# Gated-MLP down projection as Strassen products of halves, interleaved with the up projection, in a one-core decoder layer

## Chip, cores and metric

One NeuronCore of a Trainium2 chip runs the whole layer in one launch. The metric is the device time of the program in microseconds (us). TensorE is written PE, its weight loads PEld, VectorE DVE, ScalarE ACT, GpSimd POOL and SyncE SP, as in the profile.

## The reference

With DEPTH = 1 there is one layer: attention with forget gates (FoX), a layer norm, a gated MLP with a causal depthwise convolution of three taps, a second layer norm, and a gated embedding. There are 512 tokens, the model width is 1024, the inner width of the MLP 2816. Everything is float32.

```python
def conv_ffn(x, w_up, conv_w, conv_b, w_down):
    u, g = jnp.split(x @ w_up, [FFN_DIM], axis=-1)
    g = causal_dwconv(g, conv_w, conv_b)
    return (jax.nn.gelu(g, approximate=False) * u) @ w_down

x = layer_norm(ALPHA * x + fox_mixer(x, ...), ln_mix_g, ln_mix_b)
x = layer_norm(ALPHA * x + conv_ffn(x, ...), ln_ffn_g, ln_ffn_b)
x = x + sigmoid(x @ ple_w_gate + ple_b_gate) * (p @ ple_w_proj)
```

## The kernel before, in words

**Split operands.** Each float32 operand is held as two fp32r tiles, hi and lo, and each product is three matmuls into one PSUM bank: hi·hi, hi·lo, lo·hi (`three`, L93; the matmul is L98). ACT writes hi as a copy, DVE writes lo as the difference. For the weights the class `Weights` does this: `load_to` (L59) issues a DMA of a unit of 128x1024 on SP's queue into one of 4 raw buffers, `cut_to` (L70) makes `whi` on ACT (L77) and `wlo` on DVE (L78) in one of 6 pairs of buffers (`SPLIT_BUFS`), and `get` (L82) cuts some units ahead and loads some more. Units are used in the order in which they were added.

**Order of the work.** The code is written in the order of the work, and a scheduler of the framework sets the final order of each engine's instructions from it; each engine then takes its own in that order. PSUM has eight banks, given out by `bank` (L103).

**Attention** (L345 to L410) ends with the output projection. Its second half of columns (`ap`, L468 to L480) goes over four token tiles t = 0..3 of 128 tokens. After each tile DVE adds the residual and takes statistics, and `norm` (L437) normalizes the row, with POOL's power in the middle. `flip` (L449) then turns a tile: eight PE transposes into two banks `nt`, which ACT and DVE read out as `x1h` (L458) and `x1l` (L459). `flip(t - 2)` stands after tile t, so tiles 2 and 3 are still to be flipped when the loop ends. Between them and the MLP stand seven embedding products (`pl`, L496 to L503, six matmuls each), and the last two flips are laid between those.

**The MLP** (L506 to L565) goes through the 22 inner tiles f in two parts of 11. For each f it makes g and u (24 matmuls of 512 columns each), then ACT and DVE do the convolution and the gelu (L520 to L525), DVE multiplies (`e`, L527) and ACT and DVE split the result into `hh`, `hl` (L528, L529). After the 11 tiles of a part comes its down projection: for each half n of the output's columns, 11 inner tiles x 4 token tiles x 3 matmuls, `d`, each with 128 tokens as stationary operand and 512 columns moving. Four banks hold the four token tiles. `add_half` (L425) adds a bank to `y`, the running row. In the last quarter the token tile is the outer loop, and `norm` and `flip` of the second layer norm follow tile by tile.

**The gate** (L568 to L601) multiplies the flipped rows with the gate weights (`gt`), 24 matmuls for each of 8 outputs; the last one is done in two halves of 256 columns, with its embedding product last.

The body of the loop that the change replaces is this:

```python
for k in range(FH):
    for t in range(NT):
        step(t, k)
for t in range(NT):
    add_half(t, n, acc[t], part == 0)
```

Of the kernel before, what the change touches and what calls it, by code (L numbers as in the profile page):

```python
# [15 lines left out]
P = 128  # L16
S = 512
# [8 lines left out]
FH = NF // 2  # L26
# [11 lines left out]
SPLIT_BUFS = 6  # L38
# [7 lines left out]
class Weights:  # L46
# [8 lines left out]
    def add(self, src, n=UNIT, inner=None):  # L55
        self.units.append((src, n, inner))
        return len(self.units) - 1

    def load_to(self, i):  # L59
        while self.loaded < min(i, len(self.units)):  # L60
            src, n, inner = self.units[self.loaded]
# [4 lines left out]
            self.nc.sync.dma_start(v, src)  # L66
            self.raw[self.loaded] = t
            self.loaded += 1

    def cut_to(self, i):  # L70
        while self.cut < min(i, len(self.units)):
            self.load_to(self.cut + 1)
            n = self.units[self.cut][1]
            t = self.raw.pop(self.cut)
            hi = self.pool.tile([P, UNIT], F32R, tag="whi", name=f"whi{self.cut}", bufs=SPLIT_BUFS)
            lo = self.pool.tile([P, UNIT], F32R, tag="wlo", name=f"wlo{self.cut}", bufs=SPLIT_BUFS)
            self.nc.scalar.activation(hi[:, :n], t[:, :n], AF.Copy)  # L77
            self.nc.vector.tensor_sub(lo[:, :n], t[:, :n], hi[:, :n].bitcast(F32))  # L78
            self.parts[self.cut] = (hi, lo)
            self.cut += 1  # L80
# [8 lines left out]
def trunk_layer(ctx: ExitStack, tc: tile.TileContext, xT, x2d, pT, wqk, wv0, wv1, wv2, bf, wo, wup, cwb,  # L89
# [3 lines left out]
    def three(ps, whi, wlo, xhi, xlo, start, stop, weights_move=False, lo_first=False):  # L93

        pairs = ((wlo, xhi), (whi, xlo), (whi, xhi)) if lo_first else ((whi, xhi), (whi, xlo), (wlo, xhi))
        for n, (w, x) in enumerate(pairs):
            lhsT, rhs = (x, w) if weights_move else (w, x)
            nc.tensor.matmul(ps, lhsT, rhs, start=start and n == 0, stop=stop and n == 2)  # L98

    base = ctx.enter_context(tc.tile_pool(name="base", bufs=1))  # L100
    psum = ctx.enter_context(tc.tile_pool(name="psum", bufs=8, space=bass.MemoryType.PSUM))

    def bank(name):  # L103
        return psum.tile([P, 512], F32, tag="b", name=name)
# [25 lines left out]
    u_p = W.add(pT.rearrange("(k p) t -> p k t", p=P), inner=S)  # L130
    u_pl = [W.add(half_rows(wpl, 0, 2, n), inner=512) for n in range(2)]
    u_up, u_dn = [], {}
    for part in range(2):
        for f in range(part * FH, (part + 1) * FH):
            u_up.append([W.add(wup[f, s], inner=P) for s in (1, 0)])
        for n in range(2):
            k0 = part * FH
            u_dn[part, n] = []
            for j in range(0, FH, 2):
                c = min(2, FH - j)  # L140
                u_dn[part, n].append(W.add(half_rows(wdn, k0 + j, c, n), n=c * 512, inner=512))
    u_g = [[W.add(half_rows(wg, 2 * j, 2, n), inner=512) for j in range(4)] for n in range(2)]
    tl = slice(S - P, S)
# [271 lines left out]
    def row(src, name):  # L415
        t = post.tile([P, D], F32, tag="row", name=name, bufs=2)
        nc.sync.dma_start(t, src[0:1, :].to_broadcast([P, D]))
        return t

    g1, b1 = row(gm, "g1"), row(bm, "b1")  # L420
# [16 lines left out]
    def norm(t, g, b):  # L437
        mv = post.tile([P, 4], F32, tag="mv", name="mv", bufs=2)
        nc.vector.bn_aggr(mv[:, 0:2], stats.pop(t))
        nc.vector.tensor_scalar_add(mv[:, 2:3], mv[:, 1:2], EPS)  # L440
        nc.gpsimd.tensor_tensor(mv[:, 3:4], mv[:, 2:3], neghalf, op=ALU.pow)  # L441
        for n in range(2):
            c = slice(n * 512, (n + 1) * 512)
            nc.vector.scalar_tensor_tensor(y[:, t, c], y[:, t, c], mv[:, 0:1], g[:, c],
                                           op0=ALU.subtract, op1=ALU.mult)
            nc.vector.scalar_tensor_tensor(y[:, t, c], y[:, t, c], mv[:, 3:4], b[:, c],
                                           op0=ALU.mult, op1=ALU.add)
# [14 lines left out]
    x1l = post.tile([P, KD, S], F32R, tag="xl", name="x1l")  # L462

# [4 lines left out]
    for t in range(NT):  # L468
# [10 lines left out]
        if t > 1:  # L479
            flip(t - 2, x1h, x1l)  # L480
    oT.close()


    pl = base.tile([P, NT, D], F32, tag="xl", name="pl")
    W.cut_to(u_p + 3)
# [10 lines left out]
    for i, (n, t) in enumerate([(n, t) for n in range(2) for t in range(NT)][:-1]):  # L496
# [3 lines left out]
        if i == 1:  # L500
            flip(2, x1h, x1l)
        if i == 4:
            flip(3, x1h, x1l)  # L503


    hpool = ctx.enter_context(tc.tile_pool(name="hpool", bufs=1, side="right"))  # L506
    g2 = b2 = x2h = x2l = None
    for part in range(2):
        hh = hpool.tile([P, FH, S], F32R, tag="hh", name=f"hh{part}")
        hl = hpool.tile([P, FH, S], F32R, tag="hl", name=f"hl{part}")  # L510
        for fl in range(FH):
            f = part * FH + fl
            pg, pu = bank(f"g{f}"), bank(f"u{f}")
            for ps, u in ((pg, u_up[f][0]), (pu, u_up[f][1])):
                hi, lo = W.get(u, 2)
                for k in range(KD):
                    c = slice(k * P, (k + 1) * P)
                    three(ps, hi[:, c], lo[:, c], x1h[:, k, :], x1l[:, k, :], k == 0, k == KD - 1)
            a = hpool.tile([P, S], F32, tag="a", name=f"a{f}", bufs=2)
            nc.scalar.activation(a, pg, AF.Identity, bias=cw[:, f, 3:4], scale=cw[:, f, 2:3])  # L520
            nc.vector.scalar_tensor_tensor(a[:, 1:], pg[:, :S - 1], cw[:, f, 1:2], a[:, 1:],
                                           op0=ALU.mult, op1=ALU.add)
            nc.vector.scalar_tensor_tensor(a[:, 2:], pg[:, :S - 2], cw[:, f, 0:1], a[:, 2:],
                                           op0=ALU.mult, op1=ALU.add)
            nc.scalar.activation(a, a, AF.Gelu)  # L525
            e = hpool.tile([P, S], F32, tag="e", name=f"e{f}", bufs=2)
            nc.vector.tensor_mul(e, a, pu)  # L527
            nc.scalar.activation(hh[:, fl, :], e, AF.Copy)  # L528
            nc.vector.tensor_sub(hl[:, fl, :], e, hh[:, fl, :].bitcast(F32))  # L529
        if part == 1:  # L530
            g2, b2 = row(gf, "g2"), row(bff, "b2")
            x2h = post.tile([P, KD, S], F32R, tag="xh", name="x2h")
            x2l = post.tile([P, KD, S], F32R, tag="xl", name="x2l")
        for n in range(2):
            us = u_dn[part, n]
            last = part == 1 and n == 1
            acc = {}

            def step(t, k, us=us):
                hi, lo = W.get(us[k // 2])  # L540
                c = slice(k % 2 * 512, k % 2 * 512 + 512)
                tk = slice(t * P, (t + 1) * P)
                three(acc[t], hi[:, c], lo[:, c], hh[:, k, tk], hl[:, k, tk], k == 0, k == FH - 1,
                      weights_move=True)

            if not last:
                for t in range(NT):
                    acc[t] = bank(f"d{part}{n}{t}")
                for k in range(FH):
                    for t in range(NT):  # L550
                        step(t, k)
                for t in range(NT):
                    add_half(t, n, acc[t], part == 0)
                    if part == 1:
                        half_stats(t, n)
            else:
                for t in range(NT):
                    acc[t] = bank(f"d{part}{n}{t}")
                    for k in range(FH):
                        step(t, k)  # L560
                    add_half(t, n, acc[t], False)
                    half_stats(t, n)
                    norm(t, g2, b2)
                    if t > 1:
                        flip(t - 2, x2h, x2l)  # L565


    bgs = row(bg, "bgs")  # L568

    def gate(n, t, lo_c=0, w=512):  # L570
# [8 lines left out]
        e = hpool.tile([P, S], F32, tag="e", name=f"ge{n}{t}", bufs=2)[:, :w]  # L579
# [10 lines left out]
    for n in range(2):  # L590
        for t in range(NT - n):
            if n == 0 and t == 1:
                flip(2, x2h, x2l)
            if n == 0 and t == 2:
                flip(3, x2h, x2l)
            finish(n, t, gate(n, t), pl[:, t, n * 512:(n + 1) * 512])
    es = [gate(1, NT - 1, c, 256) for c in (0, 256)]
    for e, c in zip(es, (0, 256)):
        ps = bank(f"pl{NT - 1}_1{c}")[:, :256]
        embed(ps, u_p1, u_pl1, 0, P, c, 256)  # L600
        finish(1, NT - 1, e, ps, c, 256)  # L601
# [48 lines left out]
```

## Time and profile before

| | us |
|---|---|
| three timed runs | 671.20, 671.52, 672.05 |
| median | 671.52 |
| the profiled execution | 671.42 |
| its span, first to last instruction | 669.40 |
| around the span | 2.02 |

The profile is of one execution. Its page gives the busy time of each engine and the chain that ended last; the trace behind it gives each instruction with its start and duration. A matmul's record lasts longer than its slot, since matmuls are pipelined: the step from one start to the next is what one costs, and the duration (0.39 us for 512 columns) is not.

### The profile page before, as it was taken

The page shows a single profiled execution, that of the slowest core. Times are in us where ns is not written, and L with a number is a line of the kernel's source. Part 1 is how long each engine was busy: PE and PEld are TensorE (multiplying, and loading weights), DVE is VectorE, ACT ScalarE, POOL GpSimd, SP SyncE. Part 2 cuts the span into 40 slices and gives each one's busy share as a digit, 9 for nine tenths or more (in the row PEclk, how much of TensorE's full clock was granted, in tenths as well). Part 3 has the DMA queues.
Part 4 walks back from the last instruction along what each step waited for, and adds up shares of the span by engine and source line. Part 5 has one row for each costly group of instructions (what it writes and reads, how often), then busy time and mean ns, then how long its engine had stood idle before and what let it go on. Part 6 is the DMA issues. An engine that isn't in the chain of part 4 may idle for free.

```text
span 669.4 us, 8448 instructions
## 1 busy us (share of the span) xinstructions
PE 663.2 (99%) x3216; PEld 562.9 (84%) x3216; DVE 400.7 (60%) x642; ACT 290.3 (43%) x497; POOL 80.8 (12%) x78
## 2 busy tenths in 40 slices
PE   9999999999999999999999999999999999999997
PEld 7899888888888888888888888888888888888886
DVE  6774789999895796444545323254444543268763
ACT  6644687777775155343433212133343432104331
POOL 0000555444553010000000000000000000001000
PEclk9999999999999999999999999999999999999999
DMA  8533212211251317222232323233222222212411
GB/s 290 185 128 127 63 65 65 65 40 59 65 208 44 129 63 252 95 94 95 94 95 79 94 80 124 95 118 101 97 94 95 94 80 95 78 64 65 163 48 48
DMA packets 27880, 67.50 MB, mean 101 GB/s; under 512 B 2560, under 2 KB 6400, under 8 KB 27840
## 3 DMA queue, kind: packets, MB, share of 16 engines
q1 hardware_dynamic: 27840, 66.97, 30.2%
q8 instruction: 25, 0.41, 0.2%
q14 instruction: 15, 0.12, 0.1%
HBM read 64.73 MB, written 2.10 MB: 100 GB/s over the span
## 4 chain that ended last, share of the span: by engine, by line
PE 97%; ACT 1%; DMA 1%; SPq 0%; issue 0%; DVE 0%; DVEq 0%
PE d L98 18%; PE g L98 18%; PE u L98 18%; PE pp L98 13%; PE gt L98 7%; PE pv L98 6%; PE ao L98 3%; PE ap L98 3%; PE o L333 3%; PE t L320 2%; PE pl L98 2%; PE s L289 1%; PE s L291 1%; PE nt L454 1%; DMA raw<-wv 1%
## 5 line engine op out<-in xcount | busy, mean ns | idle before, releaser
L78 DVE TENSOR_TENSOR wlo<-raw,whi 128x1024 fp32r<-128x1024 f32 (+4 forms) x118 | 135.6, 1154 | 154.0 <-ACT whi L77 151.7
L77 ACT ACTIVATE whi<-raw 128x1024 fp32r<-128x1024 f32 (+4 forms) x118 | 118.4, 1005 | 207.0 <-PE g L98 82.8
L307 POOL TENSOR_SCALAR pr<-pr,rl 128x128 f32<-128x128 f32 (+1 forms) x64 | 72.7, 1153 | 134.2 <-DVE rl L303 134.2
L98 PE MATMUL d<-whi,hh 128*128 128x512 f32 x176 | 68.6, 390 | 0.0
L98 PE MATMUL d<-wlo,hh 128*128 128x512 f32 x176 | 68.5, 389 | 0.0
L98 PE MATMUL d<-whi,hl 128*128 128x512 f32 x176 | 68.5, 389 | 0.0
L98 PE MATMUL g<-x1h,whi 128*128 128x512 f32 x176 | 68.5, 389 | 0.0
L98 PE MATMUL g<-x1h,wlo 128*128 128x512 f32 x176 | 68.5, 389 | 0.0
L98 PE MATMUL u<-x1l,whi 128*128 128x512 f32 x176 | 68.5, 389 | 0.0
L98 PE MATMUL g<-x1l,whi 128*128 128x512 f32 x176 | 68.5, 389 | 0.0
L98 PE MATMUL u<-x1h,wlo 128*128 128x512 f32 x176 | 68.5, 389 | 0.0
L98 PE MATMUL u<-x1h,whi 128*128 128x512 f32 x176 | 68.5, 389 | 0.0
L441 POOL TENSOR_TENSOR mv<-mv,neghalf 128x1 f32<-128x1 f32 x8 | 7.3, 913 | 406.2 <-DVE mv L440 384.0
L98 PE MATMUL pp<-xh,wlo 128*128 128x512 f32 x128 | 50.2, 392 | 0.0
L98 PE MATMUL pp<-xl,whi 128*128 128x512 f32 x128 | 50.0, 391 | 0.0
L98 PE MATMUL pp<-xh,whi 128*128 128x512 f32 x128 | 49.9, 390 | 0.0
L527 DVE TENSOR_TENSOR e<-a,u 128x512 f32<-128x512 f32 x22 | 15.1, 688 | 43.5 <-PE u L98 41.4
L299 ACT ACTIVATE pr<-s,nm 128x128 f32<-128x128 f32 (+1 forms) x64 | 33.4, 525 | 16.9 <-DVE nm L298 14.8
L98 PEld LDWEIGHTS g<-x1l,whi 128*128 128x128 f32 x176 | 33.0, 188 | 6.9
L98 PEld LDWEIGHTS u<-x1l,whi 128*128 128x128 f32 x176 | 33.0, 188 | 6.9
L98 PEld LDWEIGHTS d<-whi,hh 128*128 128x128 f32 x176 | 33.0, 188 | 6.9
L98 PEld LDWEIGHTS g<-x1h,whi 128*128 128x128 f32 x176 | 33.0, 188 | 6.9
(129 smaller groups left out, 1254.2 us busy)
## 6 DMA issues: line engine op xcount, KB each, us to landing
raw<-wup SPq DMA_DIRECT2D x44, 512.0 KB
raw<-wdn SPq DMA_DIRECT2D x20, 512.0 KB
raw<-wqk SPq DMA_DIRECT2D x16, 512.0 KB
raw<-wo SPq DMA_DIRECT2D x8, 512.0 KB
raw<-wg SPq DMA_DIRECT2D x8, 512.0 KB
raw<-wv SPq DMA_DIRECT2D x8, 384.0 KB
y<-x2d SPq DMA_DIRECT2D x4, 512.0 KB
xraw<-xT SPq DMA_DIRECT2D x7, 256.0 KB
```

The costliest lines, as they stand in the source:

```text
L77: self.nc.scalar.activation(hi[:, :n], t[:, :n], AF.Copy)
L78: self.nc.vector.tensor_sub(lo[:, :n], t[:, :n], hi[:, :n].bitcast(F32))
L98: nc.tensor.matmul(ps, lhsT, rhs, start=start and n == 0, stop=stop and n == 2)
L289: nc.tensor.matmul(ps[:, :n], QA[:, q], KA[:, :n], start=True, stop=False)
L291: nc.tensor.matmul(ps[:, :n], qb[0:68, q], kb[0:68, :n], start=False, stop=True)
L299: nc.scalar.activation(pr[:, off:off + w], ps[:, :w], AF.Exp, bias=nm[:, i:i + 1], accum_out=ls[:, i:i + 1])
L307: nc.gpsimd.tensor_scalar_mul(pr[:, off:off + w], pr[:, off:off + w], rl[:, i:i + 1])
L320: nc.tensor.transpose(ps[:, w:w + P], pr[:, o:o + P], ident)
L333: nc.tensor.matmul(ps[:, q0:], V[:, j, h], p[:, o:o + w], start=j == 0 and n == 0, stop=j == NT - 1 and n == 1)
L441: nc.gpsimd.tensor_tensor(mv[:, 3:4], mv[:, 2:3], neghalf, op=ALU.pow)
L454: nc.tensor.transpose(ps[:, k * P:(k + 1) * P], y[:, t, (4 * n + k) * P:(4 * n + k + 1) * P], ident)
L527: nc.vector.tensor_mul(e, a, pu)
```

## The change

**Down projection.** The inner tiles are now taken in pairs (2j, 2j+1). For a pair, the rows of the activations are cut into two halves of 256 tokens and the weights into two halves of 512 output columns, so that the pair's product is a 2x2 by 2x2 product of blocks. For 9 of the 11 pairs this is done with seven block products instead of eight, in Winograd's form of Strassen's scheme. The left operands are A11, A22, A12 and four sums S1 to S4, which DVE makes in float32 from the four blocks before they are split (`operands`; split with one ACT and one DVE instruction of 128x1792). The right operands are two blocks as they are and T1 to T4, which DVE makes in the raw weight buffers before they are split (`make` in `down_units`). For T1 and T2 a block of the weights is loaded a second time into a tile `side`. The last two pairs (inner tiles 18 to 21, `REST`) are done as before.

**Order.** There are four parts of 6, 6, 6 and 4 inner tiles. The down products of a part (12 chunks: nine of two products, i.e. 12 matmuls, and three of one, i.e. 6 matmuls) are run between the g and u of the next part (`between`, `CHUNKS`): one chunk after each in parts 1 and 2, two and one by turns in part 3. The six banks x, y, z (two each) hold the running sums; some are read into `y` by DVE and go on accumulating.

**Banks.** The eight-bank pool of attention is closed after the first layer norm's loop, and a new pool with six banks and two for g and u is opened.

**The first tiles.** The embedding products no longer stand between the first layer norm and the MLP, but between the second and the gate. `flip(2)` now follows `flip(1)` at once, and g and u of tile 0 and g of tile 1 are made in halves of 256 tokens: first the tokens 0 to 255, then `flip(3)`, then the others.

**The rest.** `SPLIT_BUFS` is 5 instead of 6. `norm` works on 1024 columns in one instruction instead of two of 512. The second norm takes its token tiles in the order 2, 3, 0, 1.

```diff
-SPLIT_BUFS = 6
+PAIRS = (range(0, 3), range(3, 6), range(6, 9))
+REST = range(18, 22)
+CHUNKS = (None, (1,) * 12, (1,) * 12, (2, 1) * 4)
+HALF = S // 2
+SPLIT_BUFS = 5
...
+            for piece in [t[:, :n]] if make is None else make(t):
+                e = c + piece.shape[-1]
+                self.nc.scalar.activation(hi[:, c:e], piece, AF.Copy)
+                self.nc.vector.tensor_sub(lo[:, c:e], piece, hi[:, c:e].bitcast(F32))
+                c = e
...
+                t1, t2 = t[:, :512], side[part][:, i, :]
+                nc.vector.tensor_sub(t1, t1, t2)
+                nc.vector.tensor_sub(t2, t[:, 512:], t1)
+                return [t1, t2]
...
+            nc.vector.tensor_sub(t[:, :512], t[:, 512:], t[:, :512])
+            return [t]
...
+                nc.vector.tensor_sub(t[:, :512], t[:, :512], side[part][:, i, :])
+                return [t[:, :512]]
...
+    first.close()
+    psum.append(ctx.enter_context(tc.tile_pool(name="psum2", bufs=6, space=bass.MemoryType.PSUM)))
...
+        nc.vector.tensor_add(s1, a21, a22)
+        nc.vector.tensor_sub(s2, s1, a11)
+        nc.vector.tensor_sub(s3, a11, a21)
+        nc.vector.tensor_sub(s4, a12, s2)
+        nc.scalar.activation(hh[:, i], E[:, HALF:], AF.Copy)
+        nc.vector.tensor_sub(hl[:, i], E[:, HALF:], hh[:, i].bitcast(F32))
...
+        phases = ((ua, (("x", A11, 0), ("y", A12, 1)), (("x", 0, 0), ("y", 0, 0))),
+                  (ub, (("z", S1, 0), ("x", S2, 1)), (("x", 0, 1), ("z", 1, 1))),
+                  (uc, (("x", S3, 0), ("z", S4, 1)), (("x", 1, 1), ("z", 0, 1))),
+                  (ud, (("x", A22, 0),), (("x", 1, 0),)))
...
+    flip(2, x1h, x1l)
...
+            if f == 0:
+                a, b = slice(0, HALF), slice(HALF, S)
+                up(0, 0, a)
+                up(0, 1, a)
+                flip(3, x1h, x1l)
+                up(1, 0, a)
+                up(0, 0, b)
+                up(0, 1, b)
+                up(1, 0, b)
...
+            if f > 1:
+                up(f, 0)
+            conv(f)
+            between()
+            up(f, 1)
+            product(f, E[:, q * S:(q + 1) * S])
+            if q:
+                if part < 3:
+                    operands(hh, hl, j - 3 * part, E)
...
+            between()
+        if part < 3:
+            before = down(part, hh, hl)
```

The change moves instructions at two places that matter below. The first is PE's order where attention hands over to the MLP. Here `ap` is the last product of attention, `nt` the transposes of a flip, `pl` an embedding product, `g` the first product of the MLP. Before:

```order
L98 MATMUL ap_2582<-wlo_2465,oh 128x512
L454 MATMUL nt<-ident,y 128x128 x8
L98 MATMUL pl_0_2641<-whi_2633,whi_2476 128x512
L98 MATMUL pl_0_2641<-whi_2633,wlo_2477 128x512
L98 MATMUL pl_0_2641<-wlo_2634,whi_2476 128x512
```

And after the change:

```order
L115 MATMUL ap_2579<-wlo_2468,oh 128x512
L518 MATMUL nt<-ident,y 128x128 x16
L115 MATMUL g_2652<-x1h,whi_2479 128x256
L115 MATMUL g_2652<-x1l,whi_2479 128x256
L115 MATMUL g_2652<-x1h,wlo_2480 128x256
```

The twelve embedding matmuls that stood between the flip of tile 1 and that of tile 2 are gone: the 16 transposes are both flips, one behind the other, and the first half product of the MLP follows.

DVE's order at the same place: `y<-y,mv` are the norm of tile 2, `wlo` weight splits, `y<-y,ap` the residual of tile 3, `BN_STATS` its statistics and `x1l` what reads the banks of the flip of tile 1 out. Before:

```order
L444 SCALAR_TENSOR_TENSOR y<-y,mv,g_2407 128x512 x2
L446 SCALAR_TENSOR_TENSOR y<-y,mv,b_2409 128x512 x2
L78 TENSOR_TENSOR wlo_2638<-raw_2468,whi_2637 128x1024
L428 SCALAR_TENSOR_TENSOR y<-y,ap_2582 128x512
L78 TENSOR_TENSOR wlo_2693<-raw_2480,whi_2692 128x1024
L435 BN_STATS st_2437<-y 128x6
L459 TENSOR_TENSOR x1l<-nt,x1h 128x4x128
L439 BN_AGGR mv<-st_2437 128x2
L459 TENSOR_TENSOR x1l<-nt,x1h 128x4x128
```

And after the change:

```order
L510 SCALAR_TENSOR_TENSOR y<-y,mv,g_2414 128x1024
L94 TENSOR_TENSOR wlo_2654<-raw_2459,whi_2653 128x1024
L511 SCALAR_TENSOR_TENSOR y<-y,mv,b_2416 128x1024
L94 TENSOR_TENSOR wlo_2658<-raw_2471,whi_2657 128x1024
L496 SCALAR_TENSOR_TENSOR y<-y,ap_2579 128x512
L523 TENSOR_TENSOR x1l<-nt,x1h 128x4x128
L503 BN_STATS st_2440<-y 128x6
L523 TENSOR_TENSOR x1l<-nt,x1h 128x4x128
```

It is the same work but for the small aggregate, with the weight splits one row earlier.

The third place is DVE in part 3, between the chunks of the last Strassen part. `wlo` are weight splits, `raw` the differences that make a right operand in a raw buffer as soon as its load has landed (L174 for T3, L181 for T4), `a` the convolution, `E` the product with u, `y<-y,z` and `y<-y,x` the reading of the running sums:

```order
L94 TENSOR_TENSOR wlo107_4739<-raw107_4666,whi107_4738 128x1024
L570 SCALAR_TENSOR_TENSOR a19_4692<-g19_4657,cw_2407,a19_4692 128x511
L572 SCALAR_TENSOR_TENSOR a19_4692<-g19_4657,cw_2407,a19_4692 128x510
L94 TENSOR_TENSOR wlo108_4772<-raw108_4701,whi108_4771 128x1024
L174 TENSOR_TENSOR raw111_4776<-raw111_4776 128x512
L94 TENSOR_TENSOR wlo109_4797<-raw109_4723,whi109_4796 128x1024
L181 TENSOR_TENSOR raw113_4836<-raw113_4836,side2_4565 128x512
L577 TENSOR_TENSOR E9_4516<-a19_4692,u19_4737 128x512
L498 TENSOR_TENSOR y_2210<-y_2210,z20_4555 128x512
L94 TENSOR_TENSOR wlo110_4833<-raw110_4742,whi110_4832 128x1024
L680 TENSOR_TENSOR hl3_4515<-E9_4516,hh3_4514 128x1024
L498 TENSOR_TENSOR y_2210<-y_2210,x20_4557 128x512
```

None of these rows but the splits, the convolution and the product stood in the order before, where one row per weight unit and four per inner tile went through DVE here.

More of the change, by code (lines that the diff above doesn't have):

```diff
@@ L129, in trunk_layer @@
     u_o = [[W.add(half_rows(wo, 2 * j, 2, n), inner=512) for j in range(4)] for n in range(2)]
[L130 to L141, printed above, removed]
+    side = {}
@@ L480, in trunk_layer, with up @@
             flip(t - 2, x1h, x1l)
+    rows.close()
     oT.close()
+    first.close()
+    psum.append(ctx.enter_context(tc.tile_pool(name="psum2", bufs=6, space=bass.MemoryType.PSUM)))
+    hpool = ctx.enter_context(tc.tile_pool(name="hpool", bufs=1, side="right"))
+    ups = {}
+    def up(f, s, c=slice(0, S)):
+        if (f, s) not in ups:
+            ups[f, s] = bank(f"{'gu'[s]}{f}", *(() if f < 6 else ("gu", 2)))
+        hi, lo = W.get(u_up[f, s], 2)
+        for k in range(KD):
+            w = slice(k * P, (k + 1) * P)
+            three(ups[f, s][:, c], hi[:, w], lo[:, w], x1h[:, k, c], x1l[:, k, c], k == 0, k == KD - 1)
@@ new lines, in trunk_layer @@
+    gb = hpool.tile([P, 2, D], F32, tag="E", name="g2b2")
+    g2, b2 = row(gb[:, 0, :], gf), row(gb[:, 1, :], bff)
+    x2h = post.tile([P, KD, S], F32R, tag="xh", name="x2h")
+    x2l = post.tile([P, KD, S], F32R, tag="xl", name="x2l")
+    for g in ("hh", "hl"):
+        extra.append(hpool.tile([P, 3, UNIT], F32R, tag=g, name=f"{g}p", bufs=2))
+    for i, t in enumerate(tiles):
+        tk = slice(t * P, (t + 1) * P)
+        for n in range(2):
+            ps = bank(f"r{t}_{n}")
+            for k in range(len(REST)):
+                hi, lo = W.get(u_r[n][k // 2])
+                c = slice(k % 2 * 512, k % 2 * 512 + 512)
+                three(ps, hi[:, c], lo[:, c], hh[:, k, tk], hl[:, k, tk], k == 0, k == len(REST) - 1,
+                      weights_move=True)
+            add_half(t, n, ps, False)
+            half_stats(t, n)
+        norm(t, g2, b2)
+        if i == 0:
+            W.cut_to(u_pl[1] + 1)
+        if i > 1:
+            flip(tiles[i - 2], x2h, x2l)
@@ L494, in embed @@
             three(ps, hi[:, c], lo[:, c], ph[:, pk], plo[:, pk], k == 0, k == 1, weights_move=True)
[L496 removed]
+    for i, (n, t) in enumerate([(n, t) for n in range(2) for t in tiles][:-1]):
         ps = bank(f"pl{t}_{n}")
@@ L499, in trunk_layer @@
         nc.scalar.activation(pl[:, t, n * 512:(n + 1) * 512], ps, AF.Copy)
[L500 to L565, printed above, removed]
@@ L568, in trunk_layer @@
-    bgs = row(bg, "bgs")
+        if i == 3:
+            flip(0, x2h, x2l)
+    bgs = row(hpool.tile([P, D], F32, tag="hl", name="bgs", bufs=2), bg)
     def gate(n, t, lo_c=0, w=512):
```

183 lines of the change are left out of this document (148 added, 35 removed).

## The prediction

> **What bounds the kernel now.** I read the page first, then the chain, then PE's waits, then PE's steps.
>
> ```profile
> span 669.4 us, 8448 instructions
> PE 663.2 (99%) x3216; PEld 562.9 (84%) x3216; DVE 400.7 (60%) x642; ACT 290.3 (43%) x497; POOL 80.8 (12%) x78
> PE 97%; ACT 1%; DMA 1%; SPq 0%; issue 0%; DVE 0%; DVEq 0%
> ```
>
> ```profile
> PE warm L153 <- DVE zeros L149: 1.1, 1, 1.1
> PE pv L98 <- ACT whi L77: 0.5, 1, 0.5
> ```
>
> PE is busy for 99% of the span, the chain is PE for 97%, and the list of PE's waits has two entries, both in the first ten microseconds. A busy share can hide slow matmuls, so the step counts: in the chain, 264 down matmuls in a row, and in PE's timeline the first and the last of twelve matmuls of 256 columns at the end.
>
> ```profile
> 376.70 59.84 PE d L98 x264
> ```
>
> ```profile
> 661.86 0.28 PE L98 MATMUL gt<-whi,x2h 128*128 128x256 f32 x1
> ...
> 663.18 0.28 PE L98 MATMUL gt<-wlo,x2h 128*128 128x256 f32 x1
> ```
>
> A matmul of 512 columns costs 59.84 / 264 = 0.2267 us, one of 256 costs (663.18 - 661.86) / 11 = 0.120 us. Nothing else sets the end. So a matmul that is taken out is worth its whole step, as long as PE does not begin to wait; what the change may lose, it loses in new waits of PE.
>
> **The change part by part.** *Matmuls removed.* The down projection had 22 x 4 x 2 x 3 = 528 matmuls. A pair had 48 and now has 7 products x 2 token tiles x 3 = 42, over nine pairs 54 fewer: 54 x 0.2267 = 12.24 us. All of this lies on the path.
>
> *Matmuls halved.* g and u of tile 0 and g of tile 1 were 72 matmuls of 512 columns and are 144 of 256: 72 x (2 x 0.120 - 0.2267) = +0.96 us. The Trainium skill ("TensorE: Matmul & The Clock Gate", section "Back-to-back issue gap") gives N/2.4 + 2.5 ns for the step; by that the halves would cost 72 x (2 x 109.2 - 215.8) ns = 0.19 us, an estimate from that page. The two steps of this trace are longer than the page's 215.8 and 109.2 ns, and the measurement decides.
>
> The 42 embedding matmuls and the 64 transposes are only moved; moving them costs nothing by itself.
>
> *The handover from attention to the MLP.* This is where the embedding products covered something. PE's, ACT's and DVE's timelines:
>
> ```profile
> 244.66 1.03 PE L454 MATMUL nt<-ident,y 128*128 128x128 f32 x8
> 245.45 0.48 PE L98 MATMUL pl<-whi,whi 128*128 128x512 f32 x1
> ```
>
> ```profile
> 245.59 1.06 ACT L458 ACTIVATE x1h<-nt 128x512 fp32r<-128x512 f32 x2
> ```
>
> ```profile
> 241.18 1.41 DVE L444 SCALAR_TENSOR_TENSOR y<-y,mv,g 128x512 f32<-128x512 f32 x2
> 242.50 1.41 DVE L446 SCALAR_TENSOR_TENSOR y<-y,mv,b 128x512 f32<-128x512 f32 x2
> 243.83 1.22 DVE L78 TENSOR_TENSOR wlo<-raw,whi 128x1024 fp32r<-128x1024 f32 x1
> 244.96 0.68 DVE L428 SCALAR_TENSOR_TENSOR y<-y,ap 128x512 f32<-128x512 f32 x1
> 245.56 1.22 DVE L78 TENSOR_TENSOR wlo<-raw,whi 128x1024 fp32r<-128x1024 f32 x1
> 246.69 0.69 DVE L435 BATCH_NORM_STATS2 st<-y 128x6 f32<-128x512 f32 x1
> 247.30 0.68 DVE L459 TENSOR_TENSOR x1l<-nt,x1h 128x512 fp32r<-128x512 f32 x1
> 247.89 0.20 DVE L439 BATCH_NORM_AGGREGATE mv<-st 128x2 f32<-128x12 f32 x1
> 248.00 0.64 DVE L459 TENSOR_TENSOR x1l<-nt,x1h 128x512 fp32r<-128x512 f32 x1
> ```
>
> The flip of tile 1 is through on PE at 245.45, but DVE reads its second bank out only from 248.00 to 248.64, because the norm of tile 2, two weight splits, the residual and the statistics of tile 3 stand ahead of it in DVE's queue. Before, PE did embedding products meanwhile. Now the flip of tile 2 follows at once, and its banks are the first of the new pool. The old pool is closed with all its banks behind it, and the last reader of the old pool is that `x1l`. So PE waits. DVE's order there is the same work without the 0.11 us step of the aggregate: 241.18, two norm instructions at 1.32 each, two splits at 1.14, then 0.60 three times and 0.64 end at 248.5; with 0.1 for the signal PE goes on at 248.6. The wait is 248.6 - 245.45 = 3.15 us. Behind PE's wait all matmuls of the MLP are queued. What is late next? The readers of the flip of tile 2 only feed the second halves. The half products of g and u of tile 0 last 48 x 0.120 = 5.8 us from 249.4, so PE comes to the flip of tile 3 at 255.2; DVE has that norm done by then (from 248.5: aggregate 0.1, split 1.14, 0.1, norm 1.32, `x1l` 0.6, norm 1.32 makes 253.1). Bounds: below, only one bank is waited for and the data alone decide; PE then needs the first `x1l` at 247.3 + 0.6, after 0.8 of transposes, and waits 1.7. Above, 3.15 and one more split, 4.3. I take 3.15, since DVE's rows stand in that order.
>
> *The interleaved products.* Parts 1 and 2 last 12 x 24 x 0.2267 + 126 x 0.2267 = 93.9 us on PE, part 3 8 x 24 x 0.2267 + 126 x 0.2267 = 72.1. DVE has new work there: sums, operands, differences, 14 readings per part. In part 3 that is 39 instructions of 512 columns, 15 of 1024, 8 of the convolution, and a few of other sizes. At the steps above (0.60 and 1.14), 0.66 for the convolution and about 3 for the rest that makes 23.4 + 17.1 + 5.3 + 3 = 48.8 us, 68% of 72.1. Part 1 by the same count has about 66 us of 93.9. DVE does not become the bound by its sum. PE asks for a sum's bank, for a split or for the bank of g or u at least one chunk and one g or u (2.72 + 5.44 us) after DVE can begin on it. The tight spot is the difference in a raw buffer. It stands in DVE's queue and waits for a load that is issued only when the buffer's unit of four before is split. SP's and ACT's rows for such a load, where nothing else delayed it:
>
> ```profile
> 613.18 0.37 SPq L66 DMA_DIRECT2D raw<-wg  x1
> ```
>
> ```profile
> 617.09 1.06 ACT L77 ACTIVATE whi<-raw 128x1024 fp32r<-128x1024 f32 x1 [1.30 <-DMA raw<-wg]
> ```
>
> A load takes 3.91 us. In part 3 four such waits come one behind the other (raw buffers 108, 109, 111, 113), each behind a split of 1.14 that releases the next load. Laid end to end from the end of u of tile 18, where the split of 104 lies done, the four loads, their differences and the splits and readings between end with the reading of x about 26.1 us later, and PE wants x again after 2.72 + 5.44 + 5.44 + 5.44 + 2.72 + 5.44 = 27.2 us. That leaves 1.1 us. So the wait lies between 0 and, if each load took 1.0 more (the load of the gate's bias below was used after 4.56), 4 x 1.0 - 1.1 = 2.9 us. I take 0.3, close to what the row of 3.91 gives.
>
> ```profile
> 622.42 0.34 SPq L417 DMA_DIRECT2D bgs<-bg  x1
> ```
>
> ```profile
> 626.98 0.69 DVE L580 TENSOR_TENSOR ge<-gt,bgs 128x512 f32<-128x512 f32 x1 [0.93 <-DMA bgs<-bg]
> ```
>
> *Second norm and gate.* The four token tiles now have 24 matmuls each instead of 33, 5.44 us, and DVE must do two readings, two statistics and the norm for each (about 5.4), with three more splits. The embedding products cover this: the flip of the second tile comes 24 x 0.2267 x 4 after the first tile's start, DVE has its norm ready a microsecond or two earlier. 0, at most 1.
>
> *One pair of split buffers less.* The split of the very last weight unit now waits for the last half gate's first six matmuls. PE reaches the embedding product 18 x 0.120 = 2.16 us later; ACT needs 1.06 and DVE 1.22. With signals PE and DVE are late by 0.2, and the row by which the tail is read is DVE's last wait but one:
>
> ```profile
> 663.50 0.43 DVE L580 TENSOR_TENSOR ge<-gt,bgs 128x256 f32<-128x256 f32 x1 [2.45 <-PE gt L98]
> ```
>
> Elsewhere a unit is split four units ahead, 10 us or more, so I cost the buffer at nothing there; the cover is those units, and if it went, a split (1.14) would show at each.
>
> *Sum*, against the profiled execution: 669.40 - 12.24 + 0.96 + 3.15 + 0.3 + 0.2 = 661.8 span, and 2.02 around it makes 663.8 us. That execution took 671.42, 0.10 under the median of 671.52, which I leave out.
>
> **Rivals.** *The clock falls back in the handover.* The first matmuls of the kernel run at half speed:
>
> ```profile
> 1.10 3.17 PE L153 MATMUL warm<-zeros 128*128 128x256 bf16 x14 [1.10 <-DVE zeros L149]
> ```
>
> ```profile
> 7.41 0.29 PE L98 MATMUL pv<-whi,xl 128*128 128x272 f32 x1
> 7.65 0.39 PE L98 MATMUL pv<-wlo,xh 128*128 128x272 f32 x1
> 7.88 0.28 PE L98 MATMUL pv<-whi,xh 128*128 128x272 f32 x1
> 8.00 0.30 PE L98 MATMUL pv<-whi,xl 128*128 128x272 f32 x1
> ...
> 8.88 0.29 PE L98 MATMUL pv<-wlo,xh 128*128 128x272 f32 x1
> 9.66 0.40 PE L98 MATMUL pv<-whi,xh 128*128 128x272 f32 x1 [0.49 <-ACT whi L77]
> 9.89 0.29 PE L98 MATMUL pv<-whi,xl 128*128 128x272 f32 x1
> ```
>
> Steps of 0.23 become steps of 0.12 at 7.88, 6.8 us after the first matmul. A pause of 0.5 us does not bring them back. No row shows a pause of 3 us. If it did, between 1.7 and 3.4 us would be lost (half of 3.4 or of 6.8 us at half speed): 665.5 to 667.2. The Trainium skill (the same page, "What's actually happening") says that PE falls back to half clock after an idle window of about 3.4 us, and its table of advice ("Why this matters for your kernels") sets the limit at gaps of about 3 us. By that the wait of 3.15 is at the edge. This rule speaks against the change; no row here shows such a gap. Chance 0.13.
>
> *Loads land late in part 3.* Up to 2.9 us more, 664 to 667. For it: the extra loads of the weights. Against it: DMA is busy 34% in the stage that has the most loads. Chance 0.10.
>
> ```profile
> 254.00:374.00 120.00, 120.00 (x532) 99.41 (x531) 58.94 (x68) 47.15 (x60) 0.00 (x0) 1.00 0.34 110
> ```
>
> *No wait in the handover*, because the new pool's first banks are free earlier than I think: at best 3.15 less, 660.7. Against it speaks DVE's order. Chance 0.07.
>
> *DVE and the raw buffers fall behind for good: slower than before.* Parts 1 to 3 pass 24 + 24 + 20 = 68 units through four raw buffers, 17 turns. PE gives a turn 4 x 93.9 / 24 = 15.6 us. A turn needs 3.91 for the load, 0.69 for a difference, 1.06 and 1.22 for the split: 6.9, and whatever the instruction waits in DVE's queue. From 8.7 us of such waiting on, each turn makes PE late; at 9.4 the 17 turns cost 11 us, and the time is 675. For it: differences hold up DVE's whole queue, PE's readers included. Against it: DVE's sum leaves 30% free. Chance 0.08.
>
> **How the numbers follow.** The forecast, 663.8, has 0.62. Its own terms reach from 661.8 (handover 1.7, no other wait: 669.40 - 12.24 + 0.96 + 1.7 + 2.02) to about 665. The range goes up to 668.5, which is the clock's 667.2 and half of the late loads beside it, and leaves out the no-wait case and the slower one, 0.15 together: 661.8 to 668.5. A measurement of this kernel can tell about 0.2% (1.3 us) from no change. Faster takes the first four cases, less a little for their outer ends, 0.91; within 0.2% would need waits of 6 to 9 us, 0.02; slower 0.07.
>
> **What would show it.** PE's waits after the change: one entry of about 3.1 us, for DVE's `x1l` in the handover, and little else; the step of the matmuls of 256 columns 0.120 and of the first ones behind the wait not 0.24; 54 matmuls of 512 columns fewer; DVE's share at about 70% in the MLP; and in part 3 DVE's waits for DMA at L174 and L181, with PE's at x under 1 us. I am wrong if PE's waits sum to more than 7 us, if the wait is elsewhere than in the handover, or if DVE's queue reaches PE in parts 1 and 2.

## The result and the profile after

| | before | after |
|---|---|---|
| median of the runs, us | 671.36 | 664.54 |
| lowest to highest | 670.54 to 672.05 | 663.65 to 664.75 |
| profiled execution | 671.42 | 664.75 |
| its span | 669.40 | 663.0 |

The ratio is 0.9896, with a 95% interval of 0.9879 to 0.9913: the change makes the kernel about 7 us faster. The forecast was 663.8 in a range of 661.8 to 668.5.

First the page of the kernel after: the span, the busy times of the engines, and the chain by engine.

```profile
span 663.0 us, 8693 instructions
PE 654.0 (99%) x3234; PEld 558.0 (84%) x3234; DVE 474.0 (71%) x746; ACT 309.9 (47%) x511; POOL 85.2 (13%) x78
PE 95%; DVE 1%; ACT 1%; DMA 1%; issue 1%; SPq 0%; DVEq 0%
```

PE still carries the chain. DVE has gone from 400.7 to 474.0 us of work without becoming the bound. The list of all of PE's waits (us in total, times, the longest) has one new entry, the first:

```profile
PE nt L518 <- DVE x1l L523: 2.7, 1, 2.7
PE pv L115 <- ACT whi L93: 1.1, 2, 0.9
PE warm L223 <- DVE zeros L219: 1.1, 1, 1.1
```

It is the wait that was forecast, in the handover, for the instruction that was forecast. PE's timeline there, and DVE's:

```profile
245.25 1.03 PE L518 MATMUL nt<-ident,y 128*128 128x128 f32 x8
248.96 1.96 PE L518 MATMUL nt<-ident,y 128*128 128x128 f32 x8 [2.67 <-DVE x1l L523]
250.57 0.56 PE L115 MATMUL g<-x1h,whi 128*128 128x256 f32 x1
250.93 0.41 PE L115 MATMUL g<-x1l,whi 128*128 128x256 f32 x1
251.14 0.41 PE L115 MATMUL g<-x1h,wlo 128*128 128x256 f32 x1
...
252.42 0.28 PE L115 MATMUL g<-x1h,wlo 128*128 128x256 f32 x1
252.54 0.28 PE L115 MATMUL g<-x1h,whi 128*128 128x256 f32 x1
```

```profile
246.43 0.68 DVE L496 SCALAR_TENSOR_TENSOR y<-y,ap 128x512 f32<-128x512 f32 x1
247.03 0.68 DVE L523 TENSOR_TENSOR x1l<-nt,x1h 128x512 fp32r<-128x512 f32 x1
247.63 0.68 DVE L503 BATCH_NORM_STATS2 st<-y 128x6 f32<-128x512 f32 x1
248.23 0.67 DVE L523 TENSOR_TENSOR x1l<-nt,x1h 128x512 fp32r<-128x512 f32 x1
```

The second `x1l` begins at 248.23, takes 0.67, and PE goes on at 248.96. What was only a rival in the prediction is there too. The second flip takes 250.57 - 248.96 = 1.61 us where the one of before took 0.79, and the first matmuls of 256 columns step by 0.21 (250.93 to 251.14) before they step by 0.12 (252.42 to 252.54). The windows of the trace show the same in the granted clock (the column behind POOL's):

```profile
245.00:249.00 4.00, 1.33 (x11) 0.98 (x9) 4.00 (x8) 2.03 (x3) 0.00 (x0) 1.00 0.74 244
249.00:253.00 4.00, 4.00 (x21) 4.00 (x22) 4.00 (x6) 1.20 (x2) 1.46 (x1) 0.57 0.43 150
```

The sum closes. From the first transpose of the flip of tile 1 to PE's last matmul it was 664.62 - 244.66 = 419.96 us before and is 658.73 - 245.25 = 413.48 after, 6.48 less. The terms: 54 matmuls fewer, -12.24; halves, +0.96; the pause, 248.96 - 246.04 = +2.92, where 246.04 is the end of the first flip's slot (245.25 + 0.79); the slow flip, +0.82; the first eight matmuls of g, 252.42 - 250.57 = 1.85 instead of 0.96, +0.89; the tail, +0.2. That makes -6.45. Outside this stretch PE waited 0.6 longer for its first weights (1.1 instead of 0.5), and the end came 0.4 sooner after the last matmul.

The tail is as forecast. PE's last product is held up at two steps of 0.22 instead of 0.12:

```profile
657.45 0.28 PE L115 MATMUL pl<-whi,whi 128*128 128x256 f32 x1
657.67 0.39 PE L115 MATMUL pl<-wlo,whi 128*128 128x256 f32 x1
657.89 0.28 PE L115 MATMUL pl<-whi,whi 128*128 128x256 f32 x1
```

In part 3 DVE waits for its loads, and PE waits for nothing. First two entries of DVE's waits, then the windows of parts 1, 2 and 3 (PE, PEld and DVE are the first three busy times; the first g of part 2, 24 matmuls, lies in the first window), then DVE's reading of x at the tight spot and the matmul that wants the bank:

```profile
DVE raw L174 <- DMA raw<-wdn: 9.2, 7, 2.8
DVE raw L181 <- DMA raw<-wdn: 4.3, 3, 2.8
```

```profile
324.18:418.02 93.84, 93.84 (x416) 77.70 (x415) 64.80 (x85) 38.05 (x44) 0.00 (x0) 1.00 0.41 130
418.02:506.42 88.40, 88.40 (x392) 73.20 (x391) 60.21 (x79) 34.27 (x41) 0.00 (x0) 1.00 0.43 138
506.42:578.50 72.08, 72.08 (x320) 59.68 (x319) 50.44 (x68) 28.38 (x34) 0.00 (x0) 1.00 0.43 134
```

```profile
548.08 1.27 DVE L498 TENSOR_TENSOR y<-y,x 128x512 f32<-128x512 f32 x2
```

```profile
549.78 0.39 PE L115 MATMUL x<-whi,hh 128*128 128x512 f32 x1
```

Part 3 lasts 72.08 us, its 318 matmuls at 0.2267 make 72.09. DVE is busy for 68 to 70% of the three windows. The reading ends at 548.08 + 2 x 0.60 = 549.28, half a microsecond before PE comes.

### The profile page after: what moved, and what is told of

It reads as the page before. It is cut to its first block, busy times and chain, and to the rows that moved or that the text cites. A ratio compares the mean times of both kernels' runs of the same rounds, so it can differ in the third digit from the quotient of the medians.

```text
span 663.0 us, 8693 instructions
## 1 busy us (share of the span) xinstructions
PE 654.0 (99%) x3234; PEld 558.0 (84%) x3234; DVE 474.0 (71%) x746; ACT 309.9 (47%) x511; POOL 85.2 (13%) x78
## 4 chain that ended last, share of the span: by engine, by line
PE 95%; DVE 1%; ACT 1%; DMA 1%; issue 1%; SPq 0%; DVEq 0%
PE g L115 18%; PE u L115 18%; PE pp L115 13%; PE x L115 7%; PE gt L115 7%; PE pv L115 6%; PE z L115 4%; PE ao L115 3%; PE r L115 3%; PE o L403 3%; PE t L390 2%; PE ap L115 2%; PE y L115 2%; PE pl L115 2%; PE s L359 2%; PE s L361 1%
## 5 line engine op out<-in xcount | busy, mean ns | idle before, releaser
L93 ACT ACTIVATE whi<-raw 128x1024 fp32r<-128x1024 f32 (+5 forms) x131 | 126.3, 964 | 183.9 <-PE g L115 64.5
L94 DVE TENSOR_TENSOR wlo<-raw,whi 128x1024 fp32r<-128x1024 f32 (+5 forms) x131 | 143.2, 1099 | 67.7 <-ACT whi L93 67.1
L115 PE MATMUL g<-x1h,whi 128*128 128x512 f32 (+1 forms) x192 | 71.9, 375 | 0.0
L115 PE MATMUL g<-x1l,whi 128*128 128x512 f32 (+1 forms) x192 | 71.6, 373 | 0.0
L115 PE MATMUL g<-x1h,wlo 128*128 128x512 f32 (+1 forms) x192 | 71.6, 373 | 0.0
L115 PE MATMUL u<-x1h,whi 128*128 128x512 f32 (+1 forms) x184 | 69.9, 380 | 0.0
L115 PE MATMUL u<-x1l,whi 128*128 128x512 f32 (+1 forms) x184 | 69.9, 380 | 0.0
L115 PE MATMUL u<-x1h,wlo 128*128 128x512 f32 (+1 forms) x184 | 69.9, 380 | 0.0
L115 PEld LDWEIGHTS g<-x1h,wlo 128*128 128x128 f32 x192 | 36.5, 190 | 6.2
L115 PEld LDWEIGHTS u<-x1h,whi 128*128 128x128 f32 x184 | 34.6, 188 | 6.5
```

The lines of the kernel that those rows point to most:

```text
L93: self.nc.scalar.activation(hi[:, c:e], piece, AF.Copy)
L94: self.nc.vector.tensor_sub(lo[:, c:e], piece, hi[:, c:e].bitcast(F32))
```

## The experiments

Theory A: the 54 matmuls are worth their steps, the interleaved products cost PE nothing, and what is lost is lost in the handover, where PE waits for a pool that closes behind a late `x1l` and the pause then halves the clock. The rivals are named with each run. All times are medians beside runs of the kernel before on the same chip (671.48 for the first four, 671.66 for e5 to e8, 671.57 for e9 and e10).

| kernel | us | ratio to before, 95% interval |
|---|---|---|
| after | 664.54 | 0.9896 (0.9879 to 0.9913) |
| e1_flip_early | 661.15 | 0.9847 (0.9834 to 0.9859) |
| e2_ring | 665.99 | 0.9915 (0.9903 to 0.9928) |
| e3_ring_flip | 666.14 | 0.9923 (0.9910 to 0.9936) |
| e4_gap | 671.00 | 0.9994 (0.9985 to 1.0002) |
| e5_part3_plain | 665.42 | 0.9903 (0.9887 to 0.9918) |
| e6_block | 662.47 | 0.9860 (0.9841 to 0.9878) |
| e7_raw3 | 661.14 | 0.9839 (0.9823 to 0.9855) |
| e8_whole | 668.48 | 0.9944 (0.9926 to 0.9962) |
| e9_pause1 | 661.24 | 0.9844 (0.9829 to 0.9859) |
| e10_pause2 | 661.57 | 0.9850 (0.9834 to 0.9866) |

### e1_flip_early: is it the place of x1l?

```diff
-        if t > 1:
-            flip(t - 2, x1h, x1l)
+        if t == 2:
+            flip(0, x1h, x1l)
+            flip(1, x1h, x1l)
```

> Kernel after, but the flip of tile 1 stands right behind that of tile 0, ahead of the last 24 matmuls of ap, so that its x1l is read out under them. Theory A (PE waits for the closed pool's last reader, which is x1l of tile 1, and the pause then halves the clock for some 3.5 us): the last reader is now the residual of tile 3, 0.6 us behind the last ap; PE's wait at the flip of tile 2 falls from 2.7 to about 1.0, the 256-column steps behind it are 0.12 and not 0.21, the time falls by 3 to 3.5 us to about 661.3. Rival B (DVE's sum of work in the handover sets when g can begin, whatever the order): the wait only moves to the flip of tile 3 or to the first g, 664.5. Rival C (the slow matmuls belong to the first use of the form or of the new banks, not to the pause): the wait falls, the slow steps stay, about 662.8.

The time is 661.15, 3.4 us under the kernel after. PE's timeline:

```profile
246.94 1.06 PE L518 MATMUL nt<-ident,y 128*128 128x128 f32 x8 [1.04 <-DVE y L496]
247.76 0.36 PE L115 MATMUL g<-x1h,whi 128*128 128x256 f32 x1
247.96 0.28 PE L115 MATMUL g<-x1l,whi 128*128 128x256 f32 x1
248.08 0.28 PE L115 MATMUL g<-x1h,wlo 128*128 128x256 f32 x1
```

The releaser is now the residual of tile 3, the wait is 1.04, and the steps of the same matmuls are 0.12 from the start. So the wait hung on the order in DVE's queue and not on DVE's amount of work (against rival B), and the slow steps belonged to the pause (against rival C): the form and the place are the same here. One thing is left open. As both kernels are built, the flip of tile 2 takes over the very PSUM bank that the late reader holds (the second flip bank of tile 1 in the kernel after, the bank of the last `ap` here). So these runs do not separate a wait for the whole closed pool from a wait for that one bank.

### e2_ring and e3_ring_flip: no pool is closed

Bank by bank the attention's ring of eight is taken from two rings of six and two, which the MLP then goes on using.

```diff
+            tag, bufs = ("gu", 2) if not done and len(made) % 4 == 3 else ("b", 6)
...
-    first.close()
-    psum.append(ctx.enter_context(tc.tile_pool(name="psum2", bufs=6, space=bass.MemoryType.PSUM)))
+    done.append(True)
```

> Kernel after, but the eight banks are one pool from start to end (every fourth allocation of attention takes one of two banks of the kind that g and u use later, the others one of six), so nothing is closed; the flip of tile 1 stays where it is. Theory A: the flip of tile 2 follows at once, g begins when the first x1l of tile 1 is there, 247.7 by the rows of DVE, and the wait is about 1 us instead of 2.7; no slow steps; 661 to 661.5. Rival B: 664.5. Rival C: slow steps stay, about 662.5. If the eight banks in two rings cost attention something, attention's end comes later than 245.3.

> Both: one pool, and the flip of tile 1 ahead of the last ap. Theory A: g begins without a wait; the next in line is the norm of tile 3, which by DVE's rows is done 0.8 us later than PE wants it behind g and u of the first half; 660.5 to 661.3. Rival B: 664.5.

Both missed in time, 665.99 and 666.14. In the handover of e2 the theory holds: PE's only wait there is 0.4 us, for `x1l` as data. But attention has become slower. Its last `ap` matmul starts at 248.48, against 245.02 in the kernel after, and a new wait stands in the list:

```profile
PE t L397 <- POOL pr L384: 1.8, 3, 0.9
PE g L115 <- DVE x1l L530: 0.4, 1, 0.4
```

```profile
248.48 0.39 PE L115 MATMUL ap<-wlo,oh 128*128 128x512 f32 x1
```

The two rings give the scheduler another order in attention. These three waits are 1.8 us; where the rest of the 3.5 goes was not followed up. The trace is of the shortest of e2's four executions, 664.38 us at a granted clock of 1.000 over the span; less the 3.5 us of attention that is 660.9, about what was expected. The other three executions were granted 0.996 or 0.997 and took 1.5 to 2.1 us longer. In e3 the three at 1.000 took 664.8 to 665.4 us, the three at 0.994 to 0.997 took 666.9 to 667.9. So a fall of the clock is part of both misses; where it fell in these executions no trace shows. In e3 a wait of 1.0 us comes where it was expected, at the norm of tile 3. As a repair of the handover, one line of order (e1) did better than a new plan of the banks.

### e4_gap: a longer pause

```diff
-            nc.vector.tensor_sub(xl[:, dst[0], dst[1]], ps3, xh[:, dst[0], dst[1]].bitcast(F32))
+            for _ in range(4 if xh is x1h and t == 1 and n == 1 else 1):
+                nc.vector.tensor_sub(xl[:, dst[0], dst[1]], ps3, xh[:, dst[0], dst[1]].bitcast(F32))
```

> Kernel after, with the second read-out of x1l of tile 1 done four times instead of once, which makes PE's wait 3 x 0.60 = 1.8 us longer (about 4.5) and changes nothing else. Theory A with a clock that comes back after a fixed stretch of work: slow steps for about 3.5 us as before, time +1.8 to about 666.3. Rival D (the clock needs longer to come back after a longer pause): more than 3.5 us of slow steps, +2.5 us or more, 667 and up.

The edit did more than it should: between the four read-outs the scheduler put a weight split and the norm of tile 3, and the pause became 9.35 us, not 4.5. So the expected times no longer apply, but against the kernel after the pause is 6.7 us longer and the time 6.5, which leaves no further price for rival D. The trace agrees: after a pause 3.5 times as long, the slow stretch lasts from 254.39 to about 257.5, 3.1 us, no longer than the 3.4 us of the kernel after.

```profile
254.39 1.94 PE L518 MATMUL nt<-ident,y 128*128 128x128 f32 x8 [9.35 <-DVE x1l L524]
...
257.19 0.41 PE L115 MATMUL g<-x1h,wlo 128*128 128x256 f32 x1
257.41 0.32 PE L115 MATMUL g<-x1h,whi 128*128 128x256 f32 x1
257.57 0.29 PE L115 MATMUL g<-x1l,whi 128*128 128x256 f32 x1
```

### e5_part3_plain: what is a matmul worth?

```diff
-PAIRS = (range(0, 3), range(3, 6), range(6, 9))
-REST = range(18, 22)
-CHUNKS = (None, (1,) * 12, (1,) * 12, (2, 1) * 4)
+PAIRS = (range(0, 3), range(3, 6))
+REST = range(12, 22)
+CHUNKS = (None, (1,) * 12, (1,) * 12, (0,) * 8)
```

The ten plain inner tiles are summed as in the kernel before: the first half of the columns with the inner tile as outer loop, the second with the token tile as outer loop.

> Kernel e1_flip_early with Strassen on six pairs instead of nine: the inner tiles 12 to 21 go through the plain down projection behind the last u, nothing is interleaved in part 3. 18 matmuls of 512 columns more. Theory A (a removed matmul is worth its whole step, and the interleaved products cost PE nothing): + 18 x 0.2267 = 4.1 us, 665.2. Rival E (the interleaved part 3 has a hidden price in waits or slower steps, which goes with it): less than +3 us, under 664.2. Rival F (the plain part is dearer than its matmuls say, so that part of the measured gain was not the matmuls): over 666.

The time is 665.42, that is 4.3 us over e1 by the medians and 3.8 by the two ratios (0.9903 - 0.9847 of 671.6); 4.1 was worked out. Neither rival is needed: within some 0.3 us the interleaved part 3 has no hidden price, and the plain one is not dearer than its matmuls.

### e6_block, e7_raw3: how near is DVE to falling behind?

```diff
-CHUNKS = (None, (1,) * 12, (1,) * 12, (2, 1) * 4)
+CHUNKS = (None, (12,) + (0,) * 11, (12,) + (0,) * 11, (12,) + (0,) * 7)
```

```diff
-RAW_BUFS = 4
+RAW_BUFS = 3
```

> Kernel e1_flip_early with all twelve chunks of a part in one block behind the next part's first g, instead of one after each g and u. Same matmuls. Theory A (the interleaving is what keeps DVE and the loads off PE's path): in a block of 126 x 0.2267 = 28.6 us DVE has about 31 us of splits, differences and readings, and the loads of four raw buffers stand behind them, so PE waits 2 to 6 us in each of three blocks: 667 to 679. Rival G (buffers and DVE have slack enough; the order does not matter): under 663.

> Kernel e1_flip_early with three raw buffers instead of four: each load is issued one unit later. Theory A (part 3 is a hair from waiting for its loads, parts 1 and 2 are not): PE waits for x in part 3, 1 to 4 us, none in parts 1 and 2: 662 to 665. Rival G (slack everywhere): no new wait, 661.2. Rival H (the raw buffers are tight in all interleaved parts): more than 5 us, over 666.

Theory A missed both; rival G was right. With three raw buffers the time is that of e1, and PE has no new wait. The entry of DVE's waits at L174 has grown to 16.6 us, and even so the reading of x at the tight spot ends at 542.29 + 1.2 = 543.5, 3.2 us before PE wants the bank at 546.7:

```profile
DVE raw L174 <- DMA raw<-wdn: 16.6, 9, 4.0
```

```profile
542.29 1.28 DVE L498 TENSOR_TENSOR y<-y,x 128x512 f32<-128x512 f32 x2
```

With fewer buffers the scheduler puts the differences elsewhere in DVE's order, so a chain that is worked out for one order says little about the next. In e6 the time is 662.47, 1.3 over e1 and within what G had been given. No wait is listed in the blocks; a few steps are stretched, so that a g of 24 matmuls ahead of a block takes 5.71 us instead of 5.44. In one block DVE is busy for 25.3 us of 29.0, not for 31:

```profile
418.00:447.00 29.00, 29.00 (x129) 23.65 (x128) 25.29 (x35) 11.46 (x14) 0.00 (x0) 1.00 0.60 197
```

The count of 31 us put all splits and readings of a part into its block; the first are done ahead of it and the last behind it.

### e8_whole: what the halves cover

```diff
-                up(0, 0, a)
-                up(0, 1, a)
                 flip(3, x1h, x1l)
-                up(1, 0, a)
-                up(0, 0, b)
-                up(0, 1, b)
-                up(1, 0, b)
+                up(0, 0)
+                up(0, 1)
+                up(1, 0)
```

> Kernel e1_flip_early with g and u of tile 0 and g of tile 1 whole, behind the flip of tile 3. Theory A (the halves cost 0.96 us and cover the norm of tile 3): g begins some 7 us later, 0.96 comes back, and the pause of over 2.7 us costs about 1.5 by the clock: +6 to +8, 667 to 669. Rival I (the norm of tile 3 comes early enough once nothing stands before it): about 661 to 663.

668.48, 7.3 over e1, as theory A had it. PE waits 5.4 us for the norm of tile 3, with half clock behind it:

```profile
253.12 1.97 PE L518 MATMUL nt<-ident,y 128*128 128x128 f32 x8 [5.43 <-DVE y L511]
```

So the halves, whose own price is 0.96 us, save some 7 on balance.

### e9_pause1, e10_pause2: from which pause on does the clock fall?

Behind the residual of the last `ap` tile one more instruction reads its bank, and its result is not used.

```diff
+        for _ in range(1 if t == 3 else 0):
+            nc.vector.tensor_copy(spare, ps)
```

```diff
+        if t == 3:
+            nc.scalar.activation(spare, ps, AF.Identity, bias=y[:, t, 1023:1024])
```

> Kernel e1_flip_early with one idle copy of 512 columns on DVE that reads the bank of the last ap behind the residual, so that PE's pause at the flip of tile 2 grows from 1.04 to about 1.65 us. If the clock falls back only after some 2.5 us (theory A), the steps of 256 columns behind it stay 0.12 and the time grows by 0.6: 661.8. If it falls back from some 1.5 us on (rival J), the steps are 0.21 for 3.0 to 3.5 us and the time is 663.3.

> Kernel e1_flip_early with one idle ACT instruction of 512 columns that reads the bank of the last ap once the residual is done (its bias is a column of y), so that the pause grows to about 1.9 us. Theory A: no slow steps, 662.0. Rival J: slow steps for 3.0 to 3.5 us, 663.5.

The pauses became 1.64 and 1.67 us (1.9 was aimed at in e10), and no step is slow: the times are 661.24 and 661.57. The added 0.6 us is inside what the runs scatter.

First e9, then e10:

```profile
246.85 1.06 PE L518 MATMUL nt<-ident,y 128*128 128x128 f32 x8 [1.64 <-DVE spare L546]
247.87 0.28 PE L115 MATMUL g<-x1l,whi 128*128 128x256 f32 x1
247.99 0.28 PE L115 MATMUL g<-x1h,wlo 128*128 128x256 f32 x1
```

```profile
246.85 1.09 PE L518 MATMUL nt<-ident,y 128*128 128x128 f32 x8 [1.67 <-ACT spare L546]
247.91 0.28 PE L115 MATMUL g<-x1l,whi 128*128 128x256 f32 x1
248.03 0.28 PE L115 MATMUL g<-x1h,wlo 128*128 128x256 f32 x1
```

What the two pauses say about the limit depends on where they lie, which the last section works out.

## Why the prediction was right, step by step

- *Matmuls removed, 12.24 us.* Right. The sum of the trace closes to 0.03 us with it, and e5 gives back a third of it at the same price.
- *Halves, +0.96.* Right: 0.12 is their step wherever the clock is full, and e8 shows what they cover.
- *The handover.* Place, releaser and cause (the late reader in DVE's order) were right (e1 and e2), the pause a little shorter than forecast (2.92 from slot to slot, against 3.15).
- *The clock.* Here the prediction chose the wrong case. It said that no row shows a pause of 3 us, put the fallback at 0.13, and priced it at 1.7 to 3.4 us. It came, and cost 0.82 + 0.89 = 1.7 us by the sum above, the lower end. (Against the same rows of e1, where the first step of g is longer too, it is 1.6.) So the handover's whole price was 4.6 and not 3.15. The likeliest case with this price added would have been 665.5, and the profiled execution took 664.75: the pause was 0.2 shorter, the wait in part 3 (0.3) did not come, and 1.75 us instead of 2.02 lie around the span. The upper price of 3.4 rested on a misread row: steps of 0.23 up to 7.88 were put down to the clock. In the kernel after, matmuls of the same form step by 0.12 from 6.76 to 6.88 already and by 0.23 to 0.25 again from 7.36 to 8.07, behind a wait of only 0.19. So not all slow steps of the start are the clock's; what else slows them was not looked for.
- *Part 3.* I took 0.3, though the chain itself left 1.1 us; it was 0, with 0.5 us to spare. From the end of u of tile 18 (522.58) the reading of x was done after 26.7 us, where 26.1 were worked out from terms that are not all given. The hand-made chain found the right place, but e7 shows that it does not bound anything: one buffer less did not make PE wait.
- *DVE behind for good, chance 0.08.* Right to be small, and it was still too dear: neither the block order nor three buffers brought DVE's queue to PE.
- *Tail, +0.2.* Right.

The forecast was 0.7 us under the median and 0.95 under the profiled execution, to which its sum belongs. That it came so near is in part luck, since errors of opposite sign partly cancelled: 1.5 too little in the handover, 0.3 too much in part 3 and 0.3 too much around the span.

## What to carry over

Where PE is busy for 99%, count the matmuls, and then look only for the places where work that filled a dependency is taken away: here one such place took back 4.6 of 12.2 us. Where a pool is closed, look for the last reader of its banks: here PE waited for it. Moving that reader's input forward by one line (the flip of tile 1 ahead of the last `ap`) gave 3.4 us back, and no variant of that kernel is faster beyond the scatter. A pause of PE of some 2 us or more can have a second price behind it, which no list of waits shows: read the steps behind each wait.

## What the runs showed of the hardware

The clock's fall and return lie on a grid of 3.41 us. Windows of a quarter of a microsecond show when the granted clock changes; a window in between gives the instant by its mean. In the kernel after:

```profile
248.75:249.00 0.25, 0.04 (x1) 0.05 (x1) 0.25 (x3) 0.00 (x0) 0.00 (x0) 1.00 0.93 377
249.00:249.25 0.25, 0.25 (x2) 0.25 (x3) 0.25 (x2) 0.00 (x0) 0.00 (x0) 0.50 0.66 262
252.25:252.50 0.25, 0.25 (x3) 0.25 (x3) 0.25 (x1) 0.00 (x0) 0.00 (x0) 0.68 1.14 459
```

It falls at 249.00 and is back at 252.41 (0.16 of the 0.25 at half clock makes 0.68): 3.41 us. In e4_gap and e8_whole:

```profile
247.25:247.50 0.25, 0.00 (x0) 0.00 (x0) 0.25 (x1) 0.00 (x0) 0.00 (x0) 0.50 0.80 328
257.25:257.50 0.25, 0.25 (x3) 0.25 (x3) 0.25 (x1) 0.00 (x0) 0.00 (x0) 0.53 0.00 0
```

```profile
249.50:249.75 0.25, 0.00 (x0) 0.00 (x0) 0.25 (x2) 0.00 (x0) 0.07 (x1) 0.56 1.02 246
256.25:256.50 0.25, 0.25 (x2) 0.15 (x2) 0.20 (x1) 0.00 (x0) 0.00 (x0) 0.78 1.01 410
```

From 247.25 to 257.48 it is 10.23 us, three times 3.41; from 249.53 to 256.36 it is 6.83, twice 3.41. In e8 the clock falls 1.8 us after the long pause began (253.12 - 5.43 = 247.69), in e4 2.2 us (254.39 - 9.35 = 245.04), in the kernel after 2.7 us, just as the pause ends. The grid runs on: behind the last matmul the clock falls once more, at 662.01 in the kernel after, 667.08 in e4 and 665.96 in e8, in each 409.60 us behind its return, 120 times 3.413.

This fits a rule that looks at stretches of 3.41 us and goes by PE's idle share in each: in the stretches that ended with a fall PE had paused for 2.7, 2.2 and 2.35 us (0.51 of the short wait before it, and 1.84). The fall at a kernel's end gives the grid of the runs that had no fall before it. In e5_part3_plain it comes at 661.05, and PE was busy for 1.50 of the stretch before, so 1.92 us without work for PE was enough. In e9_pause1 it comes at 660.15; 121 stretches earlier one ends at 247.14, the pause of 1.64 us lies whole in it, and the clock stayed at 1.00:

```profile
657.63:661.05 3.42, 1.50 (x11) 1.15 (x10) 2.06 (x6) 0.42 (x1) 0.00 (x0) 1.00 0.11 38
661.00:661.25 0.25, 0.00 (x0) 0.00 (x0) 0.00 (x0) 0.00 (x0) 0.00 (x0) 0.59 0.48 172
```

```profile
243.73:247.14 3.41, 1.77 (x10) 1.23 (x9) 3.41 (x6) 2.05 (x2) 0.00 (x0) 1.00 0.19 40
```

So by this rule the limit lies between 1.64 and 1.92 us of pause in one stretch, above the 1.5 of rival J and below the 2.5 that theory A had put. e10_pause2 does not test it: counted back from its fall at 658.95, a line of the grid lies at 245.94, inside its pause of 1.67 us, with 0.75 us on one side and 0.91 on the other. The rule also says that a pause somewhat above the limit costs the clock in some executions and not in others, by where the lines happen to lie. The three waits of e2 (1.8 us in all, within 2.5 us) would be such a case. No trace of this study contradicts the rule; that it is the whole rule is not shown.

The Trainium skill ("TensorE: Matmul & The Clock Gate", section "What's actually happening") gives a free-running window of 3413 ns; by that the three distances agree. Its table of advice ("Why this matters for your kernels") warns of gaps of over about 3 us; the pause of 2.7 us here was enough, and so were 1.92 us in e5, so the measurement sets the limit lower.
